# A changed opening triple in every second unit of the feed-forward's first stage

## The chip, the cores and the metric

The kernel runs on one core of a Trainium2 chip. The metric is the device time of one execution in microseconds (us), lower is better. Times are medians of several executions; a profile shows one execution by itself.

## What is computed

A trunk of two layers on x of shape (1, 512, 1024), all in float32. Each layer has attention (eight stick-breaking heads and four differential heads on one projection) and then a dense feed-forward, which is what the change touches:

```
h = rmsnorm(x, mlp_norm[l])
u = square(relu(h @ w_ff1[l]))     # first stage: 1024 -> 4096
x = x + u @ w_ff2[l]               # second stage: 4096 -> 1024
```

## The kernel before

**Numbers.** TensorE multiplies in a reduced float32 (type F32R). For accuracy each operand is split into a rounded high half and the remainder: `whi` and `wlo` for weights, `h_hi` and `h_lo` (or `hxh` and `hxl`) for h. One product of the algorithm is then three on TensorE, a *triple*: high x high, high x low and low x high, all summed in PSUM by the helper `three` (lines 304 to 312). Line 310 multiplies the high half of the first operand `a` with the high half of `b`, line 311 its high half with the low half of `b`, line 312 its low half with the high half of `b`. In the profile a product is written out<-moving,stationary, so `X<-h_lo,whi` at line 311 streams `h_lo` through an array that holds `whi`.

**The feed-forward.** Its 4096 hidden columns are worked in four groups. The first stage of groups 1 to 3 and the second stage of all groups use a seven-product scheme for a 2 x 2 block product (Strassen's kind): seven *forms* with the names in `FORMS`, each a product of a sum of weight blocks with a sum of blocks of h. `quad_group(g, j, banks_)` runs the first stage for one half `j` of group `g`: for each of the seven forms it takes one weight tile of 128 x 1024 (a *unit*) and sends eight triples, two halves `pr` of 256 output columns by four chunks `c` of the contraction. So there are 2 layers x 3 groups x 2 halves x 7 forms = 84 units of 24 products, 2016 products, in six uninterrupted stretches of 336. Results go to the PSUM tiles X, V and Y, which the chains of forms share; ScalarE (ACT) and VectorE (DVE) take them from there.

**Walked columns.** In these products the 256 columns are not streamed in ascending order. `walked(t, 32)` views them as eight blocks of 32 and takes the blocks from the last to the first, on the moving side and in PSUM alike:

```
def walked(t, step):
    return t.rearrange("p (a b) -> p a b", b=step)[:, ::-1, :]
```

In attention, too, products of 256 columns are walked. The last products of the kernel, into the tiles Z and half, have 256 plain columns; all other products of type F32R have 256 to 512 columns. Where a block of 128 would do, the program fills it up to 256, in one place with a memset half of zeros (`zh[:, 0:128]`). Products of 128 columns occur only as transposes, which move float32 against the identity (`edge` in the profile).

**Order and buffers.** The order of units is written out in `_UNITS`. `W.next` hands out a unit's split halves and has the splitting of later units done ahead: ScalarE rounds to `whi` (line 118), VectorE makes `wlo` (line 135). A scheduler sets the final order of instructions on each engine from the program's order and its own estimates. Weights come from HBM by DMA queues of SyncE (SP) and GpSimd (POOL).

Of the kernel before, what the change touches and what calls it, by code (L numbers as in the profile page):

```python
# [17 lines left out]
P = 128  # L18
# [24 lines left out]
FORMS = ("11", "x3", "x2", "21", "x1", "x4", "22")  # L43
# [9 lines left out]
def _unit_list():  # L53
    units = []
    def qk(l, cq, ck, b):
        units.append(("p", l, cq + b * P))
        units.append(("p", l, ck + b * P))

    for l in range(L):
        for item in ORDER:  # L60
            b = int(item[1])
            if item[0] == "d":
                units.append(("x", l, b, 0))
                units.append(("x", l, b, 1))
            elif item[0] == "s":
                qk(l, SBQ, SBK, b)
            elif item[0] == "w":
                units.extend(("w", l, part) for part in range(4))
            else:
                units.extend(("v", l, SBV + b * P, half) for half in range(2))  # L70
        for half in (1, 0):
            for j in range(4):
                units.append(("o", l, half, j))
        for g in range(GROUPS):
            if g == 0:
                units.extend(("1", l, f) for f in range(2 * GP))
            else:
                units.extend(("s", l, g, j, form) for j in range(2) for form in FORMS)
            for form in FORMS2:
                for c in range(GP // 2):  # L80
                    units.append(("f", l, g, form, c))
    return units


_UNITS = _unit_list()


_INDEX = {u: i for i, u in enumerate(_UNITS)}
# [6 lines left out]
class _Weights:  # L95
# [62 lines left out]
    def next(self, kind, alone=False):  # L158
        i = self.used
        assert _UNITS[i][0] in kind  # L160
        self.used += 1
        if i > 0 and not alone:
            self.do_split(i + 2 * len(self.pools), i)
        return self.tiles.pop(i)
# [3 lines left out]
def trunk(ctx, tc, opened, xT, w, w2, w1, gfin, lamv, cos, sin, out):  # L168
    nc = tc.nc
# [70 lines left out]
    def split(hi, lo, src):  # L240
        a = nc.scalar.activation(hi, src, AF.Copy)  # L241
        nc.vector.tensor_tensor(out=lo, in0=src, in1=hi.bitcast(F32), op=ALU.subtract)  # L242
        return a
# [53 lines left out]

    def walked(t, step):
        return t.rearrange("p (a b) -> p a b", b=step)[:, ::-1, :]

    def narrow(t):
        return walked(t, 32) if t.shape[-1] == 256 and len(t.shape) == 2 else t

    def three(pt, a, b, first, last, goes_on=False, step=0):
        ah, al = a
        bh, bl = b
        if step:
            pt, bh, bl = (walked(e, step) for e in (pt, bh, bl))
        return (
            nc.tensor.matmul(pt, ah, bh, start=first, stop=False, skip_group_check=goes_on),  # L310
            nc.tensor.matmul(pt, ah, bl, start=False, stop=False, skip_group_check=goes_on),  # L311
            nc.tensor.matmul(pt, al, bh, start=False, stop=last, skip_group_check=goes_on))  # L312
# [4 lines left out]
    def wpair(u, c, n=P):  # L317
        return u[0][:, c * n : (c + 1) * n], u[1][:, c * n : (c + 1) * n]
# [27 lines left out]
    for l in range(L):  # L346
        with ExitStack() as actx:
# [49 lines left out]
            first = W.split  # L397
# [464 lines left out]
            for cost in dense(pts if l else None):  # L862
# [5 lines left out]
                while live and credit > 0:  # L868
                    c = next(at, None)
# [17 lines left out]
        with ExitStack() as fctx:  # L887
# [106 lines left out]
            def tt2(out, a, b, op):  # L994
                return nc.vector.tensor_tensor(out=out, in0=a, in1=b, op=op)
# [53 lines left out]
            def temp(k, name):  # L1049
                if k == 3:  # L1050
                    return bank("o", name)
                while ring[0] % 3 != k:
                    bank("s", "skip")
                return bank("s", name)

            def chunk(j, k):
                return x[:, ((4, 5, 6, 7), (4, 5, 0, 1))[j][k], :]

            def quad_group(g, j, banks_):
                nm = f"{l}{g}{j}"  # L1060
                X, V, Y = (temp(k, f"{n}{nm}") for k, n in zip(banks_, "XVY"))
                sx, v3 = x[:, 2, :], x[:, 3, :]
                F = [chunk(j, k) for k in range(4)]
                both = x[:, 4:8, :].rearrange("p (a b) t -> p a b t", b=2)[:, :, 0, :]
                if j:
                    both = x.rearrange("p (a b) t -> p a b t", b=4)[:, :, 0, :]
                hi, lo = ([e[:, k, :, :].rearrange("p a t -> p (a t)") for k in range(7)] for e in sides[j])
                for form in FORMS:
                    u = W.next("s")
                    to = {"x3": V, "x4": V, "21": Y}.get(form, X)  # L1070
                    h = h_forms[form]
                    for pr in range(2):
                        for c in range(4):
                            at = 512 * pr + P * c
                            three(to[:, 256 * pr : 256 * pr + 256], (u[0][:, at : at + P], u[1][:, at : at + P]),
                                  (h[0][:, c, :], h[1][:, c, :]),
                                  form in ("11", "x3") and pr == c == 0, pr == 1 and c == 3, True, 32)
                    if form == "11":
                        nc.scalar.copy(Y, X)
                    elif form == "x3":  # L1080
                        nc.scalar.copy(v3, V)
                    elif form == "x2":
                        nc.scalar.copy(sx, X)
                    elif form == "21":
                        nc.scalar.activation(F[1], Y, AF.Relu)
                        nc.scalar.activation(F[1], F[1], AF.Square)
                        split(hi[0], lo[0], F[1])
                    elif form == "x1":
                        nc.vector.scalar_tensor_tensor(
                            out=F[2], in0=X, scalar=-1.0, in1=v3, op0=ALU.mult, op1=ALU.subtract)  # L1090
                    elif form == "x4":
                        tt2(F[0], V, sx, ALU.add)
                        nc.scalar.activation(both, both, AF.Relu)
                        nc.scalar.activation(both, both, AF.Square)
                        split(hi[1], lo[1], F[2])
                        tt2(F[1], F[1], F[0], ALU.subtract)
                        tt2(F[0], F[2], F[0], ALU.subtract)
                        tt2(F[2], F[2], F[1], ALU.add)
                        split(sides[j][0][:, 3:5, :, :].rearrange("p k a t -> p (k a t)"),
                              sides[j][1][:, 3:5, :, :].rearrange("p k a t -> p (k a t)"),  # L1100
                              x[:, 4:6, :].rearrange("p c t -> p (c t)"))
                    else:
                        nc.scalar.activation(F[3], X, AF.Relu, scale=-1.0)
                        nc.scalar.activation(F[3], F[3], AF.Square)
                    if j and form in ("11", "x3", "x2"):
                        rest_of_forms(0, {"11": "21", "x3": "x2", "x2": "22"}[form])

            def rest_of_forms(j, form):
                F = [chunk(j, k) for k in range(4)]
                hi, lo = ([e[:, k, :, :].rearrange("p a t -> p (a t)") for k in range(7)] for e in sides[j])  # L1110
                if form == "21":
                    split(hi[2], lo[2], F[3])
                elif form == "x2":
                    split_less(hi[5], lo[5], F[2])
                elif form == "22":
                    tt2(F[3], F[2], F[3], ALU.subtract)
                    split(hi[6], lo[6], F[3])
# [101 lines left out]
            for g in range(GROUPS):  # L1219
# [24 lines left out]
                for form in FORMS2:  # L1244
                    total, to = SUMS[form], chains[CHAIN[form]]
                    opens = form == "11" or g == 0 and form in ("x3", "21")
                    if form == "x4" and not end:
                        to = [temp(k, f"W{l}{g}{k}") for k in (r_, s_)]
# [3 lines left out]
                    if tail and last:  # L1252
                        turned = gather(total, to)
                        to = [temp(k, f"Z{l}{k}") for k in (r_, s_)]
# [10 lines left out]
                    for n, (c, i, r, part) in enumerate(work):  # L1265
                        if c not in held:
                            held[c] = W.next("f")
                        u = held[c]
# [3 lines left out]
                        pt, b_ = to[r], wpair(u, i, 512)  # L1272
                        if part:
                            pt = halves[part - 1][:, 0:256]
# [9 lines left out]
                        if end and not last and form == "22" and n % 2:  # L1284
                            h = back(n // 2)
# [23 lines left out]
                    elif end and last and form == "x4":  # L1309
                        first = [came[0]]  # L1310
            if last:
                first += [root(2), add_half(halves[0])]
                ends, piece, whole = last_row(halves[1])
                in_order(*first, store(2, 1, False), piece, whole)
                in_order(*squares, *ends, store(2, 0, True), store_last(halves[1]))
            else:
# [6 lines left out]
                for n in range(KC):  # L1323
                    if n in (3, 5):
                        for c_ in (n + 1, n + 2):
                            h = back(c_)
# [81 lines left out]
```

## Time and profile before

| what | value |
|---|---|
| median of 3 runs | 1118.59 us (1117.84 to 1120.56) |
| the profiled execution | 1118.93 us, span 1117.2 us |
| TensorE products and weight loads | 6345 and 6345 |
| busy share PE / PEld / DVE / ACT / POOL | 99% / 87% / 81% / 62% / 14% |
| granted TensorE clock, mean | 0.999 |

The span goes from the first to the last instruction; the execution's own time has some 1.7 us around it. PE is TensorE's products, PEld its weight loads, which overlap them. Products are pipelined: the duration shown for one (0.28 us for 256 columns) is longer than the step from its start to the start of the next, and it is the steps that add up to time. Idle time of an engine off the chain that ended last costs nothing.

### The profile page before, as it was taken

Reading aid. Unit: us, or ns where it says so; the run is one execution under the profiler, and the core shown is the slowest. Engines: PE = TensorE matmul, PEld = TensorE weight load, DVE = VectorE, ACT = ScalarE, POOL = GpSimd, SP = SyncE. Lnnn points to the kernel's source line nnn. Section 1 sums busy time; section 2 is a strip of 40 time slices with the busy share of each in tenths; the row PEclk is TensorE's granted clock in tenths of the full one; section 3 lists DMA queues with packets and bytes.
Section 4 is the critical chain, followed back from the end, with each engine's and each line's share of the span. In section 5 each row is a group of like instructions: output and inputs, shape, how many; then the busy total and the mean of one; then the engine's idle time right before and its main releaser. Section 6 shows DMA issues by size and latency. Waiting matters only on the chain.

```text
span 1117.2 us, 17170 instructions
## 1 busy us (share of the span) xinstructions
PE 1109.2 (99%) x6345; PEld 970.4 (87%) x6345; DVE 908.5 (81%) x1333; ACT 689.8 (62%) x1131; POOL 152.1 (14%) x233
## 2 busy tenths in 40 slices
PE   9999999999999999999999999999999999999997
PEld 6889889888899899899878898888888998998986
DVE  7799788898668779779877897897787787797797
ACT  6447767567558457467345576775774584674765
POOL 1001343101011001001000014430011010010010
PEclk9999999999999999999999999999999999999999
DMA  7466343269787678658325654512677786787462
GB/s 243 144 189 189 114 132 106 84 221 232 170 215 182 174 201 186 190 135 211 111 76 147 190 157 131 168 59 76 209 175 185 202 187 179 184 187 206 115 132 95
DMA packets 61044, 181.25 MB, mean 162 GB/s; under 512 B 7456, under 2 KB 8736, under 8 KB 60960
## 3 DMA queue, kind: packets, MB, share of 16 engines
q1 hardware_dynamic: 50160, 141.84, 40.2%
q0 software_dynamic: 10368, 37.75, 19.5%
q8 instruction: 50, 0.82, 0.3%
q10 hardware_dynamic: 432, 0.56, 0.1%
q14 instruction: 34, 0.28, 0.1%
HBM read 150.77 MB, written 4.19 MB: 139 GB/s over the span
## 4 chain that ended last, share of the span: by engine, by line
PE 96%; DVE 2%; issue 1%; DMA 0%; ACT 0%; POOL 0%; SPq 0%; POOLq 0%; DVEq 0%; ACTq 0%
PE X L310 9%; PE X L311 9%; PE X L312 9%; PE V L311 4%; PE V L310 4%; PE V L312 3%; PE wo L310 3%; PE wo L312 3%; PE wo L311 3%; PE f L312 3%; PE f L310 3%; PE f L311 3%; PE Y L311 2%; PE Y L310 2%; PE Y L312 2%; PE W L311 1%
## 5 line engine op out<-in xcount | busy, mean ns | idle before, releaser
L118 ACT ACTIVATE whi<-q 128x1024 fp32r<-128x1024 f32 x96 | 101.7, 1059 | 107.3 <-PE X L312 38.1
L135 DVE TENSOR_TENSOR wlo<-q,whi 128x1024 fp32r<-128x1024 f32 x96 | 117.1, 1222 | 45.6 <-ACT whi L118 45.4
L135 DVE TENSOR_TENSOR wlo<-raw,whi 128x1024 fp32r<-128x1024 f32 (+1 forms) x82 | 96.8, 1187 | 6.7 <-ACT whi L118 6.4
L118 ACT ACTIVATE whi<-raw 128x1024 fp32r<-128x1024 f32 (+1 forms) x82 | 80.8, 994 | 33.4 <-issue 17.9
L310 PE MATMUL X<-whi,Ah 128*128 128x512 f32 x248 | 97.6, 394 | 0.0
L311 PE MATMUL X<-wlo,Ah 128*128 128x512 f32 x248 | 96.7, 390 | 0.0
L312 PE MATMUL X<-whi,Al 128*128 128x512 f32 x248 | 96.7, 390 | 0.0
L135 DVE TENSOR_TENSOR wlo<-waves,whi 128x1024 fp32r<-128x1024 f32 x40 | 48.8, 1221 | 16.4 <-ACT whi L118 16.3
L118 ACT ACTIVATE whi<-waves 128x1024 fp32r<-128x1024 f32 x40 | 42.3, 1057 | 29.7 <-PE X L312 18.9
L310 PEld LDWEIGHTS X<-whi,Ah 128*128 128x128 f32 x248 | 46.5, 188 | 12.1 <-DVE y L1132 1.9
L312 PEld LDWEIGHTS X<-whi,Al 128*128 128x128 f32 x248 | 46.6, 188 | 9.9
L311 PE MATMUL X<-hxl,whi 128*128 128x256 f32 x192 | 54.3, 283 | 0.0
L311 PEld LDWEIGHTS X<-wlo,Ah 128*128 128x128 f32 x248 | 46.6, 188 | 8.9
L311 PE MATMUL X<-h_lo,whi 128*128 128x256 f32 x192 | 54.3, 283 | 0.0
L310 PE MATMUL X<-h_hi,whi 128*128 128x256 f32 x192 | 53.6, 279 | 0.0
L310 PE MATMUL X<-hxh,whi 128*128 128x256 f32 x192 | 53.6, 279 | 0.0
L312 PE MATMUL X<-hxh,wlo 128*128 128x256 f32 x192 | 53.5, 279 | 0.0
L312 PE MATMUL X<-h_hi,wlo 128*128 128x256 f32 x192 | 53.5, 278 | 0.0
L310 PE MATMUL f<-h_hi,whi 128*128 128x512 f32 x128 | 50.4, 394 | 0.0
L312 PE MATMUL f<-h_hi,wlo 128*128 128x512 f32 x128 | 49.9, 390 | 0.0
L311 PE MATMUL f<-h_lo,whi 128*128 128x512 f32 x128 | 49.8, 389 | 0.0
L242 DVE TENSOR_TENSOR Al<-x,Ah 128x512 fp32r<-128x512 f32 (+1 forms) x60 | 46.5, 792 | 3.7 <-ACT Ah L241 3.5
(764 smaller groups left out, 3689.2 us busy)
## 6 DMA issues: line engine op xcount, KB each, us to landing
raw<-in_w SPq DMA_DIRECT2D x78, 512.0 KB, 3.6
q<-in_w SPq DMA_DIRECT2D x48, 512.0 KB, 4.4
q<-in_w POOLq DMA_DIRECT2D x48, 512.0 KB, 7.9
waves<-in_w SPq DMA_DIRECT2D x28, 512.0 KB, 4.5
first_a<-in_w SPq DMA_DIRECT2D x12, 512.0 KB, 5.0
first_b<-in_w SPq DMA_DIRECT2D x12, 512.0 KB, 5.2
first_c<-in_w SPq DMA_DIRECT2D x12, 512.0 KB, 4.5
first_b<-in_w POOLq DMA_DIRECT2D x12, 512.0 KB, 7.0
```

The lines of the kernel that those rows point to most:

```text
L118: return self.nc.scalar.activation(o, src, AF.Copy)
L135: self.last = h, nc.vector.tensor_tensor(out=lo[:, a:b], in0=raw[:, a:b], in1=hi[:, a:b].bitcast(F32), op=ALU.subtract)
L242: nc.vector.tensor_tensor(out=lo, in0=src, in1=hi.bitcast(F32), op=ALU.subtract)
L310: nc.tensor.matmul(pt, ah, bh, start=first, stop=False, skip_group_check=goes_on),
L311: nc.tensor.matmul(pt, ah, bl, start=False, stop=False, skip_group_check=goes_on),
L312: nc.tensor.matmul(pt, al, bh, start=False, stop=last, skip_group_check=goes_on))
```

## The change

`_opening_of` gives a unit's opening triple a kind from 0 to 7. Units are counted through the two halves `j` of a group (n from 0 to 13); those with even n have kind 0, which is the code of before. Those with odd n have kinds 1 to 7, each once in every one of the six stretches, at another form in each. Only the unit's first triple (`pr == c == 0`) is concerned, and it then goes through `begun`:

- kinds 1, 2, 3: the same three products in another order (with the operands written weight x h: high x high, low x high, high x low; high x low, high x high, low x high; low x high, high x high, high x low);
- kind 4: the first product in two pieces of 128 columns; kind 5: the third product in two pieces, each piece walked in itself;
- kind 6: the first product with plain columns; kind 7: all three with plain columns.

So 42 of the 672 triples change: 18 of them the order, 12 a split, 12 the walk.

```
+def _opening_of(l, g, j, form):
+    n = j * 7 + FORMS.index(form)
+    return (n // 2 + l * 3 + g - 1) % 7 + 1 if n % 2 else 0
...
+    def begun(kind, pt, a, b, first):
+        ah, al = a
+        todo = [(ah, b[0]), (ah, b[1]), (al, b[0])]
+        if kind == 1:
+            todo = [todo[0], todo[2], todo[1]]
+        elif kind == 2:
+            todo = [todo[1], todo[0], todo[2]]
+        elif kind == 3:
+            todo = [todo[2], todo[0], todo[1]]
+        for n, (w_, m_) in enumerate(todo):
+            whole = [(pt, m_)]
+            if kind == 4 and n == 0 or kind == 5 and n == 2:
+                whole = [(pt[:, e : e + 128], m_[:, e : e + 128]) for e in (0, 128)]
+            for k, (o, e) in enumerate(whole):
+                if not (kind == 6 and n == 0 or kind == 7):
+                    o, e = walked(o, 32), walked(e, 32)
+                nc.tensor.matmul(o, w_, e, start=first and n == k == 0, stop=False, skip_group_check=True)
...
                         for c in range(4):
                             at = 512 * pr + P * c
+                            kind = _opening_of(l, g, j, form)
+                            if kind and pr == c == 0:
+                                begun(kind, to[:, 0:256], (u[0][:, 0:P], u[1][:, 0:P]), (h[0][:, 0, :], h[1][:, 0, :]),
+                                       form in ("11", "x3"))
+                                continue
```

How the instructions stand, on TensorE, at the opening of a unit with kind 4 (first layer, group 1, half 1, form 11; the numbers are buffers, 8x32 is the walked shape). Before:

```order
L312 MATMUL X_3389<-hxh_2741,wlo_3485 128x8x32
L310 MATMUL X_3617<-h_hi,whi_3517 128x8x32
L311 MATMUL X_3617<-h_lo,whi_3517 128x8x32
L312 MATMUL X_3617<-h_hi,wlo_3518 128x8x32
L310 MATMUL X_3617<-h_hi,whi_3517 128x8x32
```

And with the change, where `three` has moved to lines 333 to 335 and `begun` sends from line 322:

```order
L335 MATMUL X_3389<-hxh_2741,wlo_3485 128x8x32
L322 MATMUL X_3617<-h_hi,whi_3517 128x4x32 x2
L322 MATMUL X_3617<-h_lo,whi_3517 128x8x32
L322 MATMUL X_3617<-h_hi,wlo_3518 128x8x32
L333 MATMUL X_3617<-h_hi,whi_3517 128x8x32
```

The first product has become two of 4 x 32 columns; the triple stands where it stood. At the other 41 openings TensorE's order differs in the same way, within the triple alone. Apart from that only a few instructions change places. On ScalarE, near the end of a stretch in the second layer (whi is a unit's high half, Ah a split result of the first stage), before:

```order
L1094 ACTIVATE x<-x 128x2x512
L118 ACTIVATE whi_10081<-q_1_8189 128x1024
L241 ACTIVATE Ah_1_8193<-x 128x512
L1103 ACTIVATE x<-X_9840 128x512
L241 ACTIVATE Ah_1_8193<-x 128x1024
```

And with the change (lines 118, 241, 1094 and 1103 have become 123, 246, 1122 and 1131):

```order
L1122 ACTIVATE x<-x 128x2x512
L246 ACTIVATE Ah_1_8199<-x 128x512
L1131 ACTIVATE x<-X_9849 128x512
L123 ACTIVATE whi_10091<-q_1_8195 128x1024
L246 ACTIVATE Ah_1_8199<-x 128x1024
```

The split of a unit that is due later now stands two steps further back. This happens at two places, a copy and a split trade places at a third, and VectorE has four such exchanges. Near the end of the second layer's feed-forward three first products of the chains V and X stand some places earlier or later. The DMA queues of SP and POOL keep their order.

## The prediction

> **What bounds the kernel now.** I read the head of the page, then the waits of TensorE, then the busy time in the six stretches that hold the changed code, and last single instructions in order of time. The page comes first (PE is TensorE's matmuls, PEld its weight loads; "x" counts instructions):
>
> ```profile
> span 1117.2 us, 17170 instructions
> PE 1109.2 (99%) x6345; PEld 970.4 (87%) x6345; DVE 908.5 (81%) x1333; ACT 689.8 (62%) x1131; POOL 152.1 (14%) x233
> PE 96%; DVE 2%; issue 1%; DMA 0%; ACT 0%; POOL 0%; SPq 0%; POOLq 0%; DVEq 0%; ACTq 0%
> ```
>
> And the list of who waited for whom (total us, times, longest), for TensorE whole:
>
> ```profile
> PE warm L225 <- POOL edge L219: 1.4, 1, 1.4
> PE p L824 <- ACT h_hi L252: 0.5, 1, 0.5
> ```
>
> TensorE is busy for 99% of the span and carries 96% of the chain that ended last. In the whole execution it waited twice for another engine, both times in the opening part and not in the feed-forward. It makes one weight load for each product (6345 of each), also where two neighbours use the same weights. So the time of the kernel here is the sum of the steps from the start of one product to the start of the next, and the question is what the 42 changed triples do to these steps. Next, the six stretches in which the changed function sends its products:
>
> ```profile
> core 0: us, PE busy (x) PEld busy (x) DVE busy (x) ACT busy (x) POOL busy (x), PEclk, DMA share, GB/s
> 319.53:359.47 39.94, 39.94 (x337) 39.94 (x336) 30.02 (x32) 29.56 (x39) 5.35 (x7) 1.00 0.77 189
> 397.86:437.80 39.94, 39.94 (x337) 39.94 (x336) 31.19 (x34) 28.67 (x37) 5.42 (x7) 1.00 0.72 182
> 476.14:516.08 39.94, 39.94 (x337) 39.94 (x336) 31.29 (x34) 28.79 (x37) 3.62 (x5) 1.00 0.63 174
> 875.91:915.85 39.94, 39.94 (x337) 39.94 (x336) 31.29 (x34) 28.78 (x37) 5.29 (x7) 1.00 0.76 188
> 954.22:994.16 39.94, 39.94 (x338) 39.94 (x336) 31.28 (x34) 28.68 (x37) 5.32 (x7) 1.00 0.75 189
> 1032.56:1072.50 39.94, 39.94 (x338) 39.94 (x336) 31.28 (x34) 28.78 (x37) 3.50 (x4) 1.00 0.50 120
> ```
>
> Each stretch has 336 products and takes 39.94 us, to the last digit the same, at a full clock (1.00) and with no idle time. One product of 256 walked columns therefore steps on by 39.94 / 336 = 118.9 ns. Six stretches with different DMA load (0.50 to 0.77) and different neighbours agree, so nothing but TensorE's own pace sets them. VectorE and ScalarE have 8.7 us or more free in each.
>
> **The change part by part.** There are 84 units in these stretches (6 stretches of 14); in 42 of them one triple of the eight is replaced. Each of the seven kinds occurs once a stretch, so six times.
>
> *Three other orders (kinds 1 to 3), 18 triples.* The same three products with the same shapes; nothing is added. What could cost is a product that reads the low half of the weights (wlo) earlier by one or two steps, some 0.24 us. Here is when one unit's two halves are made, and when its first product starts (ScalarE, VectorE, TensorE; start, duration):
>
> ```profile
> 333.87 1.06 ACT L118 ACTIVATE whi<-norms 128x1024 fp32r<-128x1024 f32 x1
> 335.77 1.22 DVE L135 TENSOR_TENSOR wlo<-norms,whi 128x1024 fp32r<-128x1024 f32 x1
> 342.35 0.28 PE L310 MATMUL V<-hxh,whi 128*128 128x256 f32 x1
> ```
>
> wlo is finished at 336.99 us and the unit opens at 342.35: 5.4 us of cover against 0.24. If that cover were gone, each of the six openings of kind 3 would wait for what VectorE is late. It isn't: cost 0. The order also changes which product follows which. The groups by line show the product with the low half of h as slightly longer than its neighbours:
>
> ```profile
> L311 PE MATMUL X<-hxl,whi 128*128 128x256 f32 x192 | 54.3, 283 | 0.0
> L310 PE MATMUL X<-hxh,whi 128*128 128x256 f32 x192 | 53.6, 279 | 0.0
> ```
>
> That 4 ns belongs to a neighbourhood (h's low half, followed by wlo) that the other orders don't have. I take 0, with ends of 4 ns less and 4 ns more for each of the 18: 0.07 us either way.
>
> *Split products (kinds 4 and 5), 12 triples.* One product of 256 columns becomes two of 128, each with a weight load of its own: 12 products and 12 loads are added. No product of this number type with 128 columns is in the trace. Two sorts of rows lie near. One is the transposes, which have 128 columns and a load of 128 each; the other is products of 512 columns:
>
> ```profile
> 100.89 0.49 PE L661 MATMUL T0d<-edge,p0d 128*128 128x128 f32 x3
> 101.21 0.60 PE L295 MATMUL rb_d<-edge,rc 128*128 128x128 f32 x4
> 101.57 0.36 PE L310 MATMUL p0u<-whi,h_hi 128*128 128x256 f32 x1
> 101.77 0.29 PE L311 MATMUL p0u<-wlo,h_hi 128*128 128x256 f32 x1
> ...
> 102.95 0.28 PE L312 MATMUL p0u<-whi,h_lo 128*128 128x256 f32 x1
> ```
>
> ```profile
> 364.00:384.00 20.00, 20.00 (x88) 16.21 (x87) 17.52 (x20) 9.16 (x11) 0.00 (x0) 1.00 0.61 172
> ```
>
> Seven transposes and one walked product take 101.77 - 100.89 = 0.88 us; less 0.119 that is 0.761, or 109 ns for a transpose. (The single start at 101.57 comes early in the record, so I take the sum over the group.) A transpose moves 128 columns and yet costs nearly what 256 do, so it is held by something that doesn't shrink with the columns; the load is the one thing that it shares with the wide product. The last row is a stretch with 512 columns alone: 20.00 / 88 = 227 ns each. From 256 to 512 columns the step grows by (227 - 118.9) / 256 = 0.42 ns a column; were that line to hold below 256, a piece would take 118.9 - 128 x 0.42 = 65 ns.
>
> So the low end for a split is 2 x 65 - 118.9 = +11 ns, the transposes' row gives 2 x 109 - 118.9 = +99 ns, and the high end, a piece that costs what 512 columns cost, is 2 x 227 - 118.9 = +335 ns. I take +99, from the row nearest in shape, since every product in the trace has its own load: 12 x 99 = +1.19 us, with ends +0.13 and +4.0.
>
> The Trainium skill (TensorE: Matmul & The Clock Gate, LDWEIGHTS) puts a load at its columns divided by 1.2, so 107 ns for 128, whatever the product's width. By it, the sum for the splits would be an estimated 12 x (213 - 119) = +1.1 us; the transposes' 109 ns agree with that rule.
>
> *Plain columns (kinds 6 and 7), 6 + 18 = 24 products.* They are neither more nor narrower, only read and written in ascending order. The end of the kernel has such products, 256 plain columns of the same number type:
>
> ```profile
> 1108.81 0.28 PE L310 MATMUL Z<-whi,Ah 128*128 128x256 f32 x1
> ...
> 1110.85 0.28 PE L312 MATMUL half<-whi,Al 128*128 128x256 f32 x1
> ```
>
> From the first to the last shown are 17 steps in 2.04 us: 120.0 ns. Plain costs 120.0 - 118.9 = 1.1 ns more, and 24 x 1.1 = +0.03 us. A plain product is followed by a walked one on the same columns in 12 places. The step from plain to walked on one tile stands here:
>
> ```profile
> 211.25 0.34 PE L692 MATMUL O0s<-turned,vs 128*128 128x384 f32 x1
> 211.43 0.34 PE L693 MATMUL O0s<-turned,vs 128*128 128x384 f32 x1
> 211.61 0.28 PE L692 MATMUL O0s<-turned,vs 128*128 128x256 f32 x1
> ```
>
> 384 plain columns step by 0.18 us to another plain product, and by 0.18 to a walked one: nothing for the change of direction, at most 10 ns by the digits shown, or 12 x 10 = 0.12 us.
>
> *What moves elsewhere.* A few steps of ScalarE and VectorE change places by one or two (a whi split later by two steps, 0.6 us each, a block of squares' differences earlier), and near the end three first products of V and X stand some places later or earlier. DMA queues (SP's and POOL's) keep their order. The ScalarE and VectorE moves lie in or just behind stretches with 8.7 us free, ahead of uses over 5 us later: cost 0. With that cover gone a delayed split would cost its 0.6 to 1.2 us once.
>
> **Sum.** 0 + 1.19 + 0.03 + 0 = +1.2 us. The profiled execution took 1118.93 us around its span of 1117.2, which is 0.3 above the median of the runs, 1118.59; the extra products weigh the same on either. 1118.59 + 1.2 = 1119.8 us, +0.11%. A measurement of this kernel can tell about 0.3%, 3.4 us, from no change: this would not be told.
>
> **The rivals.**
>
> *A narrow piece costs as much as 512 columns (slower).* For it: the program nowhere uses a product of fewer than 256 columns of this type, even where half of the 256 are zeros, which would be odd if 128 were cheap. Against it: nothing in the columns themselves asks for more passes, and the wide ones plainly run at 0.42 ns a column. Price: 12 x 335 + 0.03 = +4.05 us, 1122.6. It decides against "no change" as soon as a piece costs over 2 x piece - 118.9 = 280 ns, so 200 ns a piece. The Trainium skill (FP8 and Floating Point Precision, TensorE Precision Notes) has four passes through the array for true fp32 and a single reduced reading beside it; four passes over 128 columns would be the case of this rival, and no run here shows which one a narrow product gets.
>
> *The pace of the whole stretch falls to the plain one.* A changed opening might leave the products behind it in the 120.0 ns pace. For it: walked and plain products of one width do differ. Against it: all six stretches settle at the same 39.94 us behind different neighbours. Price: 2016 products x 1.1 = 2.2, with 1.2 on top +3.4 us, 1122.0, right at the bound.
>
> *The pace improves.* The walked products from 101.77 to 102.95 us step by (102.95 - 101.77) / 10 = 0.118 us, ten steps of 118 ns, 0.9 less than in the stretches. If every product got that, 2016 x 0.9 = 1.8 less, 1118.0 in all. To be faster by 0.3% the pace would have to fall by (3.4 + 1.2) / 2016 = 2.3 ns, to 116.6, which no long group shows.
>
> **How the numbers follow.** My forecast 0.63; the dear pieces 0.20; the pace to plain 0.08, half of it beyond the bound; the pace better 0.06, and so much better that it tells 0.03. Slower: 0.20 + 0.04 = 0.24. Faster 0.03. Within 0.3%: 0.73. The range goes from the better pace (1118.0, less 0.4, half of what the lowest of the three runs before lay under their median) to the dear pieces with as little above: 1117.6 to 1122.8. The likeliest case alone has 1118.7 (pieces at 65 ns) to 1120.2.
>
> **What would show it.** Products recorded with 128 columns, 24 of them, each with a step near 109 ns; near 65 or 227 the price of the split is wrong. A stretch should take 39.94 + 0.20 = 40.14 us, and 40.6 with dear pieces. The triples of kinds 1 to 3 should take 356 to 357 ns and that of kind 7 360. TensorE should wait for nobody in the stretches. A unit without a change that takes anything but 24 x 118.9 = 2.85 us would show that the openings set the pace of what follows, and the prediction would be wrong in its mechanism.

## The result, and the profile after

The changed kernel takes 1113.0 us (median of 3 runs, 1112.93 to 1113.04) against 1118.59 us: a ratio of 0.9949, 95% interval 0.9931 to 0.9966. It is 5.6 us faster where 1.2 us more was forecast, below the stated range. The head of its page, and the shares of the chain that ended last:

```profile
span 1111.3 us, 17194 instructions
PE 1103.6 (99%) x6357; PEld 965.1 (87%) x6357; DVE 908.3 (82%) x1333; ACT 689.2 (62%) x1131; POOL 151.9 (14%) x233
PE 98%; DVE 1%; issue 1%; DMA 0%; ACT 0%; POOLq 0%; POOL 0%; DVEq 0%; ACTq 0%
```

There are 12 products more, as the change says, TensorE is as busy as before, and the span is 5.9 us shorter. So the same engine does more work in less time. The six stretches, to be read against those of before (39.94 us each; x counts every product that touches the stretch):

```profile
318.57:357.43 38.86, 38.86 (x339) 38.86 (x338) 29.98 (x32) 29.48 (x39) 5.36 (x7) 1.00 0.77 191
395.77:435.32 39.55, 39.55 (x339) 39.55 (x338) 31.25 (x34) 28.67 (x37) 5.27 (x6) 1.00 0.75 190
473.69:512.97 39.28, 39.28 (x339) 39.27 (x338) 31.27 (x34) 28.50 (x37) 3.52 (x4) 1.00 0.63 172
872.86:911.88 39.02, 39.02 (x339) 39.02 (x338) 31.26 (x34) 28.54 (x37) 5.22 (x6) 1.00 0.76 190
950.24:989.24 39.00, 39.00 (x339) 39.00 (x338) 31.20 (x34) 28.50 (x37) 5.30 (x7) 1.00 0.77 188
1027.59:1066.45 38.86, 38.86 (x339) 38.86 (x338) 31.19 (x34) 28.70 (x37) 3.53 (x5) 1.00 0.50 123
sum 234.57, PE 234.57 PEld 234.56 DVE 186.15 ACT 172.39 POOL 28.20; mean PE 39.10 PEld 39.09 DVE 31.03 ACT 28.73 POOL 4.70
```

All are shorter, and no longer alike. Together they take 234.57 us in place of 239.64: 5.07 of the 5.9 us. Another 0.96 us was gone before the first stretch began (at 318.57 in place of 319.53 us), ahead of every changed instruction. That part cannot be put down to the change: in the nine experiments below that leave everything ahead of the first stretch as it was, the stretch begins anywhere from 318.55 to 319.41 us.

Where in a stretch the time went shows in the starts of the units, here in the first stretch (start, duration; line 322 is a changed opening, line 333 an unchanged one):

```profile
318.57 0.28 PE L333 MATMUL X<-h_hi,whi 128*128 128x256 f32 x1
...
321.41 0.28 PE L322 MATMUL V<-hxh,whi 128*128 128x256 f32 x1
...
324.16 0.28 PE L333 MATMUL X<-hxh,whi 128*128 128x256 f32 x1
...
326.88 0.28 PE L322 MATMUL Y<-h_lo,whi 128*128 128x256 f32 x1
...
337.76 0.33 PE L322 MATMUL X<-h_hi,whi 128*128 128x128 f32 x2
...
340.59 0.28 PE L333 MATMUL V<-hxh,whi 128*128 128x256 f32 x1
...
343.31 0.28 PE L322 MATMUL X<-hxh,whi 128*128 128x256 f32 x1
...
346.25 0.28 PE L333 MATMUL Y<-h_hi,whi 128*128 128x256 f32 x1
...
349.11 0.28 PE L322 MATMUL X<-h_hi,whi 128*128 128x256 f32 x1
...
351.86 0.28 PE L333 MATMUL V<-h_hi,whi 128*128 128x256 f32 x1
...
354.58 0.28 PE L322 MATMUL X<-hxh,whi 128*128 128x256 f32 x1
...
357.43 0.40 PE L333 MATMUL X<-whi,Ah 128*128 128x512 f32 x1
```

Read the differences. The first unit takes 2.84 us, as before. The second opens with kind 1 and takes 2.75. The third, whose code is unchanged, takes 2.72, and so does everything up to 337.76 (326.88 to 337.76 is four units in 10.88 us). 2.72 us for 24 products are 113.3 ns each, the *quick* pace from here on; before, every unit took 2.85, 118.9 ns a product, the *slow* one. The opening of kind 5 at 343.31 ends it: that unit takes 2.94, and the next, unchanged, 2.86. Kind 6 at 349.11 brings the quick pace back (2.75, then 2.72), and kind 7 at 354.58 ends it again (2.85). So the same walked products run at two paces, and an opening sets the pace of the units behind it.

The same reading of all six stretches gives one rule without an exception (the pace is that of the products behind the opening; "not met" means that no such opening came at that pace):

| kind | what is changed | from the slow pace | from the quick pace |
|---|---|---|---|
| 1 | high x high, low x high, high x low | to quick, 6 of 6 | not met |
| 2, 3 | the other two orders | stays slow, 3 of 3 | stays quick, 9 of 9 |
| 4 | first product split | to quick, 3 of 3 | stays quick, 3 of 3 |
| 5 | third product split | stays slow, 1 of 1 | to slow, 5 of 5 |
| 6 | first product plain | to quick, 6 of 6 | not met |
| 7 | all three plain | not met | to slow, 6 of 6 |

Every stretch begins slow, also where the one before ended quick: the products of 512 columns between them do not carry the pace on. The long records of the low half of h, 283 ns before, are shorter now too:

```profile
L334 PE MATMUL X<-hxl,whi 128*128 128x256 f32 x180 | 50.2, 279 | 0.0
```

### The profile page after: what moved, and what is told of

It is laid out like the page before. It is cut to its first block, busy times and chain, and to the rows that moved or that the text cites. A ratio compares the mean times of both kernels' runs of the same rounds, so it can differ in the third digit from the quotient of the medians.

```text
span 1111.3 us, 17194 instructions
## 1 busy us (share of the span) xinstructions
PE 1103.6 (99%) x6357; PEld 965.1 (87%) x6357; DVE 908.3 (82%) x1333; ACT 689.2 (62%) x1131; POOL 151.9 (14%) x233
## 4 chain that ended last, share of the span: by engine, by line
PE 98%; DVE 1%; issue 1%; DMA 0%; ACT 0%; POOLq 0%; POOL 0%; DVEq 0%; ACTq 0%
PE X L333 9%; PE X L334 9%; PE X L335 9%; PE V L334 4%; PE V L333 4%; PE V L335 3%; PE wo L334 3%; PE wo L333 3%; PE wo L335 3%; PE f L333 3%; PE f L334 3%; PE f L335 3%; PE Y L334 2%; PE Y L333 2%; PE Y L335 2%; PE W L333 1%
## 5 line engine op out<-in xcount | busy, mean ns | idle before, releaser
L334 PE MATMUL X<-h_lo,whi 128*128 128x256 f32 x180 | 50.3, 279 | 0.0
L334 PE MATMUL X<-hxl,whi 128*128 128x256 f32 x180 | 50.2, 279 | 0.0
L333 PE MATMUL X<-h_hi,whi 128*128 128x256 f32 x180 | 50.1, 278 | 0.0
L333 PE MATMUL X<-hxh,whi 128*128 128x256 f32 x180 | 50.0, 278 | 0.0
L335 PE MATMUL X<-h_hi,wlo 128*128 128x256 f32 x180 | 49.9, 277 | 0.0
L335 PE MATMUL X<-hxh,wlo 128*128 128x256 f32 x180 | 49.9, 277 | 0.0
```

## Experiments

Each was timed in turns with the kernel before on one chip, in four groups (before: 1118.43, 1118.5, 1118.14 and 1118.21 us). The first four change nothing but which unit gets which kind.

**Kind 1 once in each stretch.** The last line of `_opening_of` becomes

```
-    return (n // 2 + l * 3 + g - 1) % 7 + 1 if n % 2 else 0
+    return 1 if n == 1 else 0
```

> Changed: only the second unit of each stretch opens with the order high x high, low x high, high x low (kind 1); the other 83 units are those of before. Theory of the held pace: the walked products have two paces, 118.9 and 113.3 ns a product, this opening switches to the quick one, and it holds until something switches it back or the stretch ends. A stretch then takes 2.85 + 2.75 + 12 x 2.72 = 38.2 us in place of 39.94, and the kernel is 6 x 1.7 = 10.3 us faster (ratio 0.991) with 6 changed triples. Rival, a local gain (a changed opening helps its own unit and the next): 0.11 + 0.13 us a stretch, 1.4 us in all (ratio 0.9987).

1107.93 us, ratio 0.9906 (0.9893 to 0.9920). The first and the last stretch:

```profile
318.55:356.79 38.24, 38.24 (x338) 38.23 (x336) 29.83 (x32) 29.21 (x39) 5.27 (x6) 1.00 0.73 191
...
1023.32:1061.55 38.23, 38.23 (x337) 38.23 (x336) 31.09 (x34) 28.43 (x37) 3.49 (x4) 1.00 0.50 121
```

38.24 us, the 38.2 of the held pace; 36 fewer changed triples give about twice the gain. The rival of a local gain is ruled out.

**Kinds 5 and 7 alone.**

```
-    return (n // 2 + l * 3 + g - 1) % 7 + 1 if n % 2 else 0
+    kind = (n // 2 + l * 3 + g - 1) % 7 + 1 if n % 2 else 0
+    return kind if kind in (5, 7) else 0
```

> Changed: only the openings of kind 5 (third product split) and kind 7 (three plain products) are left, 12 triples; all other units are those of before. Theory of the held pace: these two never switch to the quick pace, so every stretch stays at 118.9 ns and gets only the price of one split, 39.94 + 0.1 = 40.0 us; the kernel is 0.5 us slower (ratio 1.0005). Rival (any changed opening loosens the products behind it): a part of the gain stays, 2 of 7 of 5 us, so about 1.4 us faster.

1119.03 us, ratio 1.0005 (0.9996 to 1.0014), and every stretch slow, 0.10 us over 39.94. Kind 7, which the changed kernel never sent at the slow pace, leaves it slow here, 6 of 6. One of the stretches:

```profile
318.74:358.78 40.04, 40.04 (x338) 40.03 (x337) 30.03 (x32) 29.54 (x39) 5.33 (x7) 1.00 0.77 190
```

**Kinds 2 and 3 alone**, in all 42 places:

```
-    return (n // 2 + l * 3 + g - 1) % 7 + 1 if n % 2 else 0
+    return 2 + n // 2 % 2 if n % 2 else 0
```

> Changed: all units with odd n open with kind 2 or 3 in turn (the other two orders), 42 triples; nothing is split or plain. Theory of the held pace: these two leave the pace as they find it, so each stretch stays slow, 39.9 us, and the time is that of before (ratio 1.000), though seven times as many triples are changed as with kind 1 alone. Rival (any change of order loosens the stream): most of the 10 us of kind 1.

1118.10 us, ratio 1.0000 (0.9991 to 1.0009), 39.92 us a stretch:

```profile
318.79:358.71 39.92, 39.92 (x337) 39.91 (x336) 30.03 (x32) 29.54 (x39) 5.33 (x7) 1.00 0.75 187
```

42 changed triples gain nothing, where 6 of another order took 10 us away.

**On and off.**

```
-    return (n // 2 + l * 3 + g - 1) % 7 + 1 if n % 2 else 0
+    return {1: 1, 7: 7}.get(n, 0)
```

> Changed: in each stretch the second unit opens with kind 1 and the eighth with kind 7 (three plain products). Theory of the held pace: units 2 to 7 are quick, units 8 to 14 slow again, so a stretch takes 2.85 + 2.75 + 5 x 2.72 + 2.85 + 6 x 2.85 = 39.2 us and the kernel is 6 x 0.8 = 4.7 us faster (ratio 0.996). Rival, local gain: 1.4 us. Rival, the quick pace belongs to some units whatever was before them: the same units are quick as with kind 1 alone.

1113.54 us, ratio 0.9956 (0.9942 to 0.9970); a stretch takes the 39.2 us expected:

```profile
319.23:358.39 39.16, 39.16 (x338) 39.16 (x336) 30.01 (x32) 29.64 (x39) 5.37 (x7) 1.00 0.76 191
```

The pace can be put on and taken off at will. With these four, the held pace is shown.

**Order 1 in all 672 triples** (the second and third product trade places in the stretches; no `begun`). For the stretches `three` becomes

```
     nc.tensor.matmul(pt, ah, bh, start=first, ...)
-    nc.tensor.matmul(pt, ah, bl, start=False, stop=False, ...)
-    nc.tensor.matmul(pt, al, bh, start=False, stop=last, ...)
+    nc.tensor.matmul(pt, al, bh, start=False, stop=False, ...)
+    nc.tensor.matmul(pt, ah, bl, start=False, stop=last, ...)
```

> Changed: all eight triples of all 84 units have the order high x high, low x high, high x low; nothing is split or plain. If the order itself is what makes products quick, the stretches take 336 x 113.3 = 38.1 us from the start and the kernel is 11 us faster. If the change from one order to another is what switches the pace, nothing switches here: the stretches stay near 39.9 us, and the time is that of before.

1115.26 us, ratio 0.9970 (0.9959 to 0.9982): neither. In the profiled execution a stretch takes 39.07 us, and the rest of the span 1.7 us more than before. The stretch is quick from the first unit on until TensorE has to wait, for ScalarE to copy X, before the tenth unit's first product (TensorE's products there, and the row of the waits of its loads):

```profile
343.39 0.28 PE L312 MATMUL V<-hxh,wlo 128*128 128x256 f32 x1
343.50 0.28 PE L313 MATMUL V<-hxl,whi 128*128 128x256 f32 x1
343.84 0.39 PE L311 MATMUL X<-hxh,whi 128*128 128x256 f32 x1
344.06 0.28 PE L312 MATMUL X<-hxh,wlo 128*128 128x256 f32 x1
344.18 0.28 PE L313 MATMUL X<-hxl,whi 128*128 128x256 f32 x1
344.30 0.28 PE L311 MATMUL X<-hxh,whi 128*128 128x256 f32 x1
```

```profile
PEld X L311 <- ACT Y L1084: 1.5, 6, 0.3
```

The step from 343.50 to 343.84 is 0.34 us in place of 0.11, the next, to 344.06, is 0.22, and from there on the steps are 0.12: slow for the remaining five units, in all six stretches (the six waits of that row). So neither the order nor the units own a pace. The quick one ended at a pause of 0.2 us each time, and the same order that began quick went on slow. That the pause is what ended it is the nearest reading; no run made a pause by itself.

**Kind 1 at the first unit.**

```
-    return (n // 2 + l * 3 + g - 1) % 7 + 1 if n % 2 else 0
+    return 1 if n == 0 else 0
```

> Changed: in each stretch only the first unit (not the second) opens with kind 1. If the opening triple can switch the pace at any place, the first unit is quick too and a stretch takes 14 x 2.72 = 38.1 us, 0.1 less than with the second unit (1107.2 in all). If the pace must first have settled to the slow one before it can be switched, nothing switches, a stretch stays at 39.9 and the time is that of before.

1107.57 us, ratio 0.9903 (0.9886 to 0.9919), the lowest median of all, though within the noise of the others near 1107.9:

```profile
319.20:357.29 38.09, 38.09 (x337) 38.09 (x336) 29.82 (x32) 29.20 (x39) 5.28 (x6) 1.00 0.73 187
```

38.09 us is 14 units of 2.72: the switch works from the stretch's first triple.

**Plain columns in the stretches, with the changed second unit.** Kind 1 at n == 1, and

```
-                    o, e = walked(o, 32), walked(e, 32)
+                    pass
...
-    form in ("11", "x3") and pr == c == 0, pr == 1 and c == 3, True, 32)
+    form in ("11", "x3") and pr == c == 0, pr == 1 and c == 3, True,0)
```

> Changed: every product of the six stretches has plain columns, and the second unit of each opens with kind 1 (plain as well). If the quick pace needs the walk, all products stay at the plain pace of 120.0 ns: a stretch takes 336 x 120 = 40.3 us and the kernel is 2.3 us slower than before (ratio 1.002). If the switch alone makes the quick pace, a stretch takes 38.2 us and the kernel is 10 us faster.

1107.96 us, ratio 0.9906 (0.9891 to 0.9921), 38.10 us a stretch. The number is near that of the second case, but its reason does not hold: the first unit, ahead of the switch, takes 2.74 us and is quick already. The next experiment leaves the switch out.

**Plain columns, no opening changed** (no `begun`; the call of `three` alone is edited).

```
-    form in ("11", "x3") and pr == c == 0, pr == 1 and c == 3, True, 32)
+    form in ("11", "x3") and pr == c == 0, pr == 1 and c == 3, True, 0)
```

> Changed: all products of the six stretches have plain columns, and no opening is changed. If the stretch runs at the quick pace by itself once nothing is walked (the kernel with plain columns and a changed second unit was quick before that unit came), a stretch takes 38.1 us and the kernel is 11 us faster than before (ratio 0.990). If the plain pace is the 120.0 ns of the end of the kernel, a stretch takes 40.3 us and the kernel is 2.3 us slower.

1107.77 us, ratio 0.9905 (0.9888 to 0.9921). One stretch, and then the plain products at the end of this same kernel:

```profile
318.94:357.04 38.10, 38.10 (x338) 38.10 (x336) 29.82 (x32) 29.23 (x39) 5.29 (x6) 1.00 0.75 191
```

```profile
1098.52 0.28 PE L310 MATMUL half<-whi,Ah 128*128 128x256 f32 x1
...
1099.48 0.28 PE L312 MATMUL half<-whi,Al 128*128 128x256 f32 x1
```

Unwalked, the stretch settles at the quick pace by itself (113.4 ns a product in the mean); 256 plain columns at the end of the kernel step by 0.96 / 8 = 120 ns still. The walk, which looked like a gain of 1.1 ns from the row at the end, costs 5.5 here when nothing switches the pace.

**One walked triple in plain stretches** (the opening of the eighth unit; kind 8 is in `begun` the usual order, walked).

```
-    return (n // 2 + l * 3 + g - 1) % 7 + 1 if n % 2 else 0
+    return 8 if n == 7 else 0
...
-    form in ("11", "x3") and pr == c == 0, pr == 1 and c == 3, True, 32)
+    form in ("11", "x3") and pr == c == 0, pr == 1 and c == 3, True, 0)
```

> Changed: all products of the stretches have plain columns, but the three of the opening triple of the eighth unit are walked (kind 7 the other way round). If what flips the pace is the change between plain and walked columns, the stretch falls from 113.3 to the plain pace of 120 ns there: 7 x 2.72 + 7 x 2.88 = 39.2 us a stretch, 4.4 us faster than before in all. If only walked products have a slow pace in the stretch, it stays quick: 38.1 us, 11 us faster.

1107.78 us, ratio 0.9906 (0.9892 to 0.9921), 38.1 us a stretch: it stays quick. Three walked products among plain ones do not end the quick pace, though three plain ones among walked ones do (kind 7). So the mixing alone is not what ends it.

**No walk anywhere** (and no `begun`).

```
-        return t.rearrange("p (a b) -> p a b", b=step)[:, ::-1, :]
+        return t
```

> Changed: no product of the kernel is walked, in the feed-forward and in attention. If plain columns are quick wherever products of 256 columns follow each other undisturbed, the short groups in attention (about 150 products, 6 to 30 in a row) gain up to 5 ns each, 0.7 us, beside the gain of the stretches. If short groups never settle, the time is that of the kernel with plain stretches alone.

1107.91 us, ratio 0.9906 (0.9891 to 0.9920): no difference from plain stretches alone that can be told.

**Walked 512 columns.** Kind 1 at the second unit, and the second stage's `three` with `step` 32, without and with the order of kind 1 in each form's second triple (`swap`, as in the kernel with all triples reordered).

```
-    opens and n == mine[0] and part < 2, n == mine[-1], not opens)
+    opens and n == mine[0] and part < 2, n == mine[-1], not opens, 0 if part else 32, False)
...
+    opens and n == mine[0] and part < 2, n == mine[-1], not opens, 0 if part else 32, n == 1 and not part)
```

> Changed: kind 1 at the second unit of each stretch as in the first experiment, and the products of 512 columns of the feed-forward's second stage are walked in blocks of 32 (before: plain, 227 ns). If the walk only helps where loads and columns take alike (256), these products stay at 227 ns and the time is that of the first experiment, 1107.9. If a walked 512 has a quick pace as well, 5.6 ns less, it gains 5.6 ns for each of some 1300 products, 7 us.

> Changed: as the kernel before in this call, and the second triple of each form of the second stage has the order of kind 1. If a walked 512 has two paces like a walked 256 and needs a switch, this one is up to 7 us faster than 1107.9; if the step of 512 columns has no second pace, the time is that of the first experiment.

1114.51 us (0.9966, 0.9953 to 0.9979) and 1114.28 us (0.9964, 0.9951 to 0.9977), both over 6 us slower than kind 1 alone. A window of 20 us now holds 87 of these products instead of 88:

```profile
361.00:381.00 20.00, 20.00 (x87) 16.02 (x86) 17.71 (x20) 10.21 (x13) 0.88 (x1) 1.00 0.69 183
```

The walk costs there: between waits the steps average 232 to 233 ns in both kernels, where plain 512 columns take 226.7, and the changed order made no second pace. The 5 to 7 ns are about the distance of the two paces of 256 columns; whether walked 512 columns stand in a slow pace of their own stays open.

These two kernels show one thing more. The first unit of a stretch is unchanged in them (kind 1 comes at the second). Behind plain 512 columns, walked units of the usual order began slow in all 36 stretches of the kernels above; behind walked 512 columns five of the twelve stretches began quick. Two of the stretches of the second kernel, one that began slow and one that began quick:

```profile
396.78:435.02 38.24, 38.24 (x337) 38.23 (x336) 31.01 (x34) 28.42 (x37) 5.30 (x6) 1.00 0.73 188
474.18:512.27 38.09, 38.09 (x338) 38.09 (x336) 31.01 (x34) 28.45 (x37) 3.52 (x4) 1.00 0.61 168
```

So the opening triple is not the only thing that sets the pace: the products ahead of the stretch do as well.

## Why the prediction was wrong

*The step that failed* is the tacit one under the sum: that products which the change doesn't touch keep their 118.9 ns. From six stretches of 39.94 us, equal to the last digit, I read that "nothing but TensorE's own pace sets them". That no other engine set them is right, but it does not follow that TensorE has only this one pace there. The equal stretches had equal code; they showed that this pace is reached each time, not that it is a limit. In the changed kernel 50 of the 84 units ran quick, unchanged ones among them. The stretches took 5.1 us less in all; the 12 splits added about 12 x 0.113 = 1.4 us to that, so the term that stood at 0 was about -6.4 us, an estimate from these two figures.

*The rival nearest to what happened*, "the pace improves", stood in the text. Its condition for a gain that tells was right: the pace had to fall "to 116.6, which no long group shows", and the mean after is 115.7 ns (39.10 us a stretch for 338 products). Its weight, 0.03, was too small, and its mechanism was another: it put all products at 118 ns, near the slow pace, where the runs show two paces and a switch between them. The prediction's own sign of a wrong mechanism, an unchanged unit that takes anything but 2.85 us, is what the profile showed: 2.72.

*Three other orders: 0.* Right for kinds 2 and 3 (ratio 1.0000), wrong for kind 1, which took 10.5 us away with 6 triples. From the slow pace its own three products take 0.36 us, as forecast; the gain is all in the products behind them. The wait for wlo never came in the stretches.

*Split products: +0.099 us each.* The unit of kind 4 from 337.76 to 340.59 takes 2.83 us between units of 2.72: +0.11. The total was near, but the working behind it was partly luck: the pieces do not step by 109 ns each. The recorded steps are 0.06 us for the first piece, 0.11 for the second and 0.17 for the product behind them, together 0.34 us where two undivided products take 0.23. The dear piece (+0.335 us a split) did not come. By the Trainium skill (TensorE: Matmul & The Clock Gate, LDWEIGHTS) a load of 128 columns takes an estimated 107 ns, which lies 6 ns under the measured 113. The runs cannot tell the price of a load from that of one more step at the quick pace.

*Plain columns: +1.1 ns.* The row at the end of the kernel was the wrong neighbour. It has the same type, width and order of columns with other operands, and it gave 120.0 where plain stretches give 113.4. Among walked products the plain ones acted as switches (kinds 6 and 7), which the term did not have.

*Steps elsewhere: 0.* Right; neither products nor weight loads waited for another engine in the changed kernel's stretches. The "twice" in the prediction's reading counts the waits of products alone: weight loads of the kernel before waited at more places, all outside the stretches (the most for VectorE's y: five waits, 1.9 us).

What stays open is why an opening switches the pace. Kinds 1, 4 and 6 have in common neither an order nor a shape, and kinds 4 and 5 differ only in which product is split. The pause before the tenth unit and the quick starts behind walked 512 columns speak for a state that the stream of loads and products carries along, but no run here showed that state itself.

## What to carry to other kernels

On a bound engine a perfectly repeatable step is not proof of a floor. The trace before could hardly warn of it: outside the stretches it has some 90 steps of 112 to 115 ns between products of 256 columns, but nearly all stand alone and never three in a row. Where long runs of equal products settle slowly, a change of one triple at the start, or plain addressing, costs a few lines to try; test it on one opening at a time, since a mixture of openings that switch the pace on and off gave here half of what one alone did. A price taken from the same shape with other operands can mislead: plain columns were priced 6.6 ns too dear here.

## What the runs showed of the hardware

- Walked products of 256 columns with 128 x 128 weights ran at two paces in the stretches, 113.3 and 118.9 ns (2.72 and 2.85 us for 24), at a full clock (1.00) in both. Settled (with kind 1 at the first unit), the quick pace has steps of 113 or 114 ns alone; the slow one, in the kernel before, has steps of 116 to 119 ns and one of 124 or 125 in every six. The quick pace held over 300 products. It ended at a pause of 0.2 us in six of six stretches, and it was not carried through plain products of 512 columns to the next stretch.
- The Trainium skill (TensorE: Matmul & The Clock Gate, Back-to-back issue gap) gives one gap of 262 cycles for 256 columns, an estimated 109 ns, for a product by itself, and says that in a stream of loads and products both set the spacing. The measured paces are 4 and 10 ns above that gap, and that there are two is not in that rule.
- Walking 512 columns in blocks of 32 made the kernel 6.6 us slower than without (1114.51 against 1107.93, where the kernel before took 1118.50 and 1118.43).
